# Odd-layer values in six chunks of 512 weight columns instead of eight of 384

## The chip, the cores and the metric

The kernel runs on one core of one Trainium2 chip. The metric is the device time of one execution in microseconds (us), the median of three timed runs. The engines are named as in the profile: PE is TensorE's matmuls, PEld its weight loads, DVE is VectorE, ACT ScalarE, POOL GpSimd, SP the engine that issues nearly all DMAs.

## The reference

A two-layer encoder trunk on 256 tokens of width 1024, float32. The even layer has neighbourhood and latent attention, the odd layer a mixture of dilated windows; each is followed by a squared-ReLU MLP. Cut to the odd layer, which is the one that changes:

```python
def odd_mixer(xn, w_in, w_o, cos_f, sin_f):
    b, s, _ = xn.shape
    hcat = (xn @ w_in).reshape(b, s, DIL_GROUPS, 3, DIL_HEADS, HEAD_DIM)
    q = apply_rope(hcat[:, :, :, 0], cos_f, sin_f)
    k = apply_rope(hcat[:, :, :, 1], cos_f, sin_f)
    v = hcat[:, :, :, 2]
    return dilated_attention(q, k, v) @ w_o
```

`DIL_GROUPS` is 3 (window patterns), `DIL_HEADS` 16 heads of 64. For each head, `dilated_attention` takes a softmax in each of the three groups over the keys of that group's window and combines the three by their softmax denominators, which is the same as one softmax over all three groups' scores side by side.

## The kernel before

**Products in two parts.** A float32 weight comes by DMA into a tile `raw` (`load_weight`, L138). ScalarE rounds it into `whi` (L176) and VectorE writes the rest `raw - whi` into `wlo` (L177), in four pieces per weight. Activations are held as such pairs too. A product is then three matmuls, high times high, high times low, low times high (`mm3`, L179 to L182), or two, where high and low of the activation lie side by side as 512 columns (`mm2`, L184 to L187: one of 512 columns and one of 256). The weights of the whole trunk stand in one list, `specs`; `weight()` (L167) hands out the next one, loads four ahead and splits two ahead. There are four `raw` buffers and three pairs `whi`/`wlo`.

**The odd layer** (`odd`, L782) works in eight units of two heads. For each unit u:

- `qk_steps` (L823): three weights of 1 MB, b = 0, 1, 2: queries and keys of group 0; then queries of groups 1 and 2; then their keys. Each b has four steps (f, half) of four `mm2` pairs; a bank `acc` of the accumulation memory holds the result of one f, 128 weight columns, and `joined` (L191: a copy on ScalarE, an add on VectorE, L193 and L194) takes it out. Behind the fourth step stands `rope`: four small DMAs on SP swap the halves, and VectorE multiplies and adds (L847 to L853). The results are the tiles `q0` (group 0), `q12` and `k12`.
- `value_steps` (L798): two weights of 768 KB. Per block of 128 tokens 24 matmuls of 384 columns (8 parts of the depth, three matmuls each) sum up in one bank; `out` (L813) takes the 384 columns out, scaled: 128 by VectorE into `v0`, twice 128 by ScalarE into `v12`.
- `attention` (L863): `scores` puts the group 0 scores (`two_heads`, L201, with `q0`) and those of groups 1 and 2 (L878, with `q12` and `k12`) into four banks `w`, then, for each of four pairs (i, j) of token block and head, reduces and subtracts on VectorE (L886), takes exponentials and scales on ScalarE (L890, L892). `turn` (L895) transposes the probabilities `pp` on TensorE (L899, three matmuls) and copies them out as `pts` (L901, on ScalarE or VectorE).
- `mix` (L906): the transposed probabilities times `v0` and `v12` (L914, L919), into one bank `acc`, split into `oa` or `ob` for the output product.

The loop over u from 2 to 7 (L936) weaves the product steps of unit u with the attention of unit u - 1, into which the mix of unit u - 2 is put behind the scores: twelve steps of queries and keys, then four of values, and beside them scores, two empty steps, and the four turns with an empty step behind each. `weave` (L203) spreads the second list over the first in proportion to their lengths. "Unit u's loop" is below what the weave of unit u's products holds, with the attention of unit u - 1. Unit 0 has no attention beside it; in unit 1's loop the attention of unit 0 starts three steps late; the attention of unit 7 stands beside the output product (L943), which opens four banks `acc` at once.

**What sets the order.** The code lists the steps, but a scheduler lays down each engine's queue when the program is built: it keeps the order of the code where an instruction is ready by its own estimate, and puts later ones ahead of one that it takes to be late. Each engine then runs its queue in that order, waiting on counts of the other engines. There are four banks `acc` and four banks `w`; a new tile takes a bank whose last reader is through.

Of the kernel before, what the change touches and what calls it, by code (L numbers as in the profile page):

```python
# [39 lines left out]
WPARTS = 4  # L40
NORM_PRIO = 300


@with_exitstack
def trunk(ctx, tc, a, out):
# [82 lines left out]
    for u in range(8):  # L128
        ov = [(a["w_ov"][u, j], 4 * 384) for j in range(2)]
        oqk = [(a["w_oqk"][u, j], WCH) for j in range(3)]  # L130
        specs.extend(oqk + ov if u else ov + oqk)
# [47 lines left out]
    def mm3(o, sh, sl, mh, ml, first, last):  # L179
        nc.tensor.matmul(o, sh, mh, start=first, stop=False)  # L180
        nc.tensor.matmul(o, sh, ml, start=False, stop=False)  # L181
        nc.tensor.matmul(o, sl, mh, start=False, stop=last)  # L182
# [29 lines left out]
    def tok(t):  # L212
        return slice(t * P, (t + 1) * P)
# [568 lines left out]
    def odd(op, xT, s):  # L782
# [8 lines left out]
        def unit_tiles(u):  # L791
            d = {}
            for n, shape, dt in (("q0", [P, 2, 2, T], F32R), ("q12", [P, 2, T], F32), ("k12", [P, 2, T], F32),
                                 ("v0", [P, NT, P], F32), ("v12", [P, 4, P], F32)):
                d[n] = op.tile(shape, dt, tag=n, name=n, bufs=2)
            return d

        def value_steps(d):  # L798

            wt, acc = [], {}  # L800

            def gemm(i, half):
                if len(wt) <= half:
                    wt.append(weight())
                if half == 0:
                    acc[i] = bank("acc")
                pq = acc[i]
                wh, wl = wt[half]
                for k in range(4):
                    ws = slice(k * 384, k * 384 + 384)  # L810
                    kk = 4 * half + k
                    mm3(pq[:, 0:384], xh[:, kk, tok(i)], xl[:, kk, tok(i)], wh[:, ws], wl[:, ws], kk == 0, kk == KT - 1)
            def out(i):  # L813
                pq, ri = acc[i], column(r[0], i)
                nc.vector.tensor_scalar(d["v0"][:, i, :], pq[:, 0:P], ri, None, ALU.mult)
                for c in range(2):
                    rows = slice(64 * c, 64 * c + 64)
                    nc.scalar.activation(d["v12"][0:64, 2 * i + c, :], pq[rows, P:2 * P], AF.Copy, scale=ri[rows])
                    nc.scalar.activation(d["v12"][64:P, 2 * i + c, :], pq[rows, 2 * P:3 * P], AF.Copy, scale=ri[rows])

            return [lambda i=i, h=h: gemm(i, h) for i in range(NT) for h in range(2)], [lambda i=i: out(i) for i in range(NT)]
# [34 lines left out]

        def all_values(d):
            g, o = value_steps(d)
            return [g[0], lambda: run_all([g[1], o[0]]), g[2], lambda: run_all([g[3], o[1]])]

# [44 lines left out]

        def mix(u, d, out_tag):  # L906
            pvo = bank(out_tag)
            for i in range(NT):
                pts = [turned.pop((u, i, j)) for j in range(2)]
                at = i * P  # L910
                for kk in range(NT):
                    for j in range(2):
                        cs = slice(64 * j, 64 * j + 64)
                        nc.tensor.matmul(pvo[cs, tok(i)], d["v0"][:, kk, cs], pts[j][:, kk, :], start=kk == 0, stop=False)  # L914
                for c in range(2):
                    qs = slice(64 * c, 64 * c + 64)
                    for j in range(2):
                        cs = slice(64 * j, 64 * j + 64)
                        nc.tensor.matmul(pvo[cs, at + 64 * c:at + 64 * c + 64], d["v12"][:, 2 * i + c, cs], pts[j][:, 2, qs],  # L919
                                         start=False, stop=c == 1)  # L920
            split(*halves(mixed[u // 4][:, u % 4]), pvo[:, 0:T])

        d, nd = unit_tiles(0), unit_tiles(1)
        v0, v_out = value_steps(d)
        run_all(v0)
        r = [rstd(s)]
# [7 lines left out]
        run_all(first[2:])  # L934
        weave(qk_steps(nd) + all_values(nd), attention(0, d, lambda: None, 3), 3)
        for u in range(2, 8):  # L936
            pd, d, nd = d, nd, unit_tiles(u)
            side = attention(u - 1, d, lambda: mix(u - 2, pd, "acc"))

            weave(qk_steps(nd) + all_values(nd), side + [lambda: mix(6, d, "acc")] if u == 7 else side)  # L940
        accs, wo = open_accs(), {}
        side = attention(7, nd, lambda: None) + [lambda: mix(7, nd, "w")]
        weave([f for k in range(6) for f in out_steps(accs, mixed, wo, k)], side)  # L943
# [54 lines left out]
def _layout(i):  # L998
# [56 lines left out]
```

## Time and profile before

| what | value |
|---|---|
| median of three runs | 745.56 us (745.47 to 745.57) |
| profiled execution | 745.33 us, its span 743.5 us |
| granted TensorE clock, mean | 0.998 |
| odd layer's units 2 to 6 | from 350.5 to 499.5 us of the span, 29.8 us each |
| loads of value weights | 16 of 768 KB, 4.7 us each to landing |
| loads of query and key weights | 24 of 1 MB, 5.1 us each to landing |

A row of groups reads: line, engine, operation, written tile, read tiles, shape, count; then busy time, mean of one in ns, and idle time ahead of it with what ended it. A row of the timeline reads: start and length in us, engine, line, operation, tiles, shape, count, and in brackets the engine's idle time just before and what ended it. A row of the windows reads: the stretch, its length, then busy time of PE, PEld, DVE, ACT and POOL with their counts, granted clock, share of the DMA engines, GB/s. Matmul records overlap, since the next one starts before the last has drained.

### The profile page before, as it was taken

Reading aid. Unit: us, or ns where it says so; the run is one execution under the profiler, and the core shown is the slowest. Engines: PE = TensorE matmul, PEld = TensorE weight load, DVE = VectorE, ACT = ScalarE, POOL = GpSimd, SP = SyncE. Lnnn points to the kernel's source line nnn. Section 1 sums busy time; section 2 is a strip of 40 time slices with the busy share of each in tenths; the row PEclk is TensorE's granted clock in tenths of the full one; section 3 lists DMA queues with packets and bytes.
Section 4 is the critical chain, followed back from the end, with each engine's and each line's share of the span. In section 5 each row is a group of like instructions: output and inputs, shape, how many; then the busy total and the mean of one; then the engine's idle time right before and its main releaser. Section 6 shows DMA issues by size and latency. Waiting matters only on the chain.

```text
span 743.5 us, 12706 instructions
## 1 busy us (share of the span) xinstructions
PE 735.2 (99%) x4764; PEld 644.6 (87%) x4764; DVE 550.1 (74%) x1248; ACT 463.4 (62%) x1038; POOL 6.1 (1%) x16
## 2 busy tenths in 40 slices
PE   8999999999999999999999999999999999999996
PEld 6898998888888888989899899898998888888885
DVE  6699849666666666998888988888869665665664
ACT  6679977454454556758676766867667554554541
POOL 0100000000000000000000000000000000000000
PEclk9999999999999999999999999999999999999999
DMA  8866334554464554575655455456653655555401
GB/s 283 340 210 223 114 114 160 183 224 173 171 222 174 174 191 149 189 242 171 199 207 183 164 194 196 165 177 225 216 199 121 218 171 201 176 191 192 178 26 56
DMA packets 28108, 136.88 MB, mean 184 GB/s; under 512 B 4496, under 2 KB 7056, under 8 KB 14992
## 3 DMA queue, kind: packets, MB, share of 16 engines
q1 hardware_dynamic: 27760, 135.81, 53.0%
q8 instruction: 37, 0.61, 0.3%
q10 hardware_dynamic: 288, 0.28, 0.1%
q14 instruction: 23, 0.19, 0.1%
HBM read 127.68 MB, written 1.05 MB: 173 GB/s over the span
## 4 chain that ended last, share of the span: by engine, by line
PE 95%; DMA 1%; issue 1%; DVE 0%; SPq 0%; ACT 0%; POOLq 0%; POOL 0%; DVEq 0%
PE w L186 16%; PE acc L180 14%; PE acc L181 14%; PE acc L182 14%; PE acc L186 12%; PE w L187 8%; PE acc L187 6%; PE w L201 1%; PE w L899 1%; PE w L714 1%; PE acc L914 1%; DMA raw<-in_w_v 1%; PE w L729 1%; PE w L878 1%; DMA raw<-in_w_c 1%
## 5 line engine op out<-in xcount | busy, mean ns | idle before, releaser
L177 DVE TENSOR_TENSOR wlo<-raw,whi 128x512 fp32r<-128x512 f32 (+3 forms) x488 | 304.1, 663 | 75.6 <-ACT whi L176 74.0
L176 ACT CAST whi<-raw 128x512 fp32r<-128x512 f32 (+3 forms) x488 | 264.2, 602 | 81.1 <-issue 70.3
L186 PE MATMUL w<-xT,whi 128*128 128x512 f32 x512 | 179.3, 394 | 0.0
L186 PE MATMUL acc<-xT,whi 128*128 128x512 f32 x384 | 137.3, 401 | 0.0
L187 PE MATMUL w<-xT,wlo 128*128 128x256 f32 x512 | 132.8, 280 | 0.0
L186 PEld LDWEIGHTS w<-xT,whi 128*128 128x128 f32 x512 | 93.6, 187 | 18.3
L187 PEld LDWEIGHTS w<-xT,wlo 128*128 128x128 f32 x512 | 96.1, 188 | 5.5
L187 PE MATMUL acc<-xT,wlo 128*128 128x256 f32 x384 | 99.8, 280 | 0.0
L180 PE MATMUL acc<-whi,h 128*128 128x512 f32 x250 | 98.4, 393 | 0.0
L181 PE MATMUL acc<-wlo,h 128*128 128x512 f32 x250 | 97.8, 391 | 0.0
L182 PE MATMUL acc<-whi,h 128*128 128x512 f32 x250 | 97.4, 390 | 0.0
L186 PEld LDWEIGHTS acc<-xT,whi 128*128 128x128 f32 x384 | 70.0, 188 | 12.7
L193 ACT COPY up<-w 128x256 f32<-128x256 f32 x64 | 23.9, 374 | 88.4 <-PE w L186 88.4
L187 PEld LDWEIGHTS acc<-xT,wlo 128*128 128x128 f32 x384 | 72.2, 188 | 3.7
L194 DVE TENSOR_TENSOR up<-up,w 128x256 f32<-128x256 f32 x64 | 26.8, 419 | 63.0 <-ACT up L193 62.2
L180 PE MATMUL acc<-whi,xT 128*128 128x384 f32 (+2 forms) x160 | 56.5, 353 | 0.6 <-ACT whi L176 0.6
L181 PE MATMUL acc<-wlo,xT 128*128 128x384 f32 (+2 forms) x160 | 56.0, 350 | 0.3 <-DVE wlo L177 0.3
L182 PEld LDWEIGHTS acc<-whi,h 128*128 128x128 f32 x250 | 46.9, 188 | 10.2
L181 PEld LDWEIGHTS acc<-wlo,h 128*128 128x128 f32 x250 | 47.0, 188 | 9.8
L182 PE MATMUL acc<-whi,xT 128*128 128x384 f32 (+2 forms) x160 | 55.4, 346 | 0.0
L180 PEld LDWEIGHTS acc<-whi,h 128*128 128x128 f32 x250 | 46.9, 188 | 9.1
L181 PEld LDWEIGHTS acc<-wlo,xT 128*128 128x128 f32 x160 | 30.2, 189 | 3.1 <-DVE wlo L177 2.1
(195 smaller groups left out, 1043.6 us busy)
## 6 DMA issues: line engine op xcount, KB each, us to landing
raw<-in_w SPq DMA_DIRECT2D x64, 1024.0 KB, 4.8
raw<-in_w_oqk SPq DMA_DIRECT2D x24, 1024.0 KB, 5.1
raw<-in_w_ov SPq DMA_DIRECT2D x16, 768.0 KB, 4.7
sw<-qk SPq DMA_DIRECT2D x96, 64.0 KB, 3.2
raw<-in_w_qk SPq DMA_DIRECT2D x4, 1024.0 KB, 11.0
raw<-in_w_oe SPq DMA_DIRECT2D x4, 1024.0 KB, 5.7
raw<-in_w_oo SPq DMA_DIRECT2D x4, 1024.0 KB, 5.5
bias<-in_rpb SPq DMA_DIRECT2D x8, 256.0 KB, 4.2
```

The source lines that it names most:

```text
L176: a = nc.scalar.copy(hi, src).ins
L177: return a, (eng or nc.vector).tensor_tensor(lo, src, hi.bitcast(F32), op=ALU.subtract).ins
L180: nc.tensor.matmul(o, sh, mh, start=first, stop=False)
L181: nc.tensor.matmul(o, sh, ml, start=False, stop=False)
L182: nc.tensor.matmul(o, sl, mh, start=False, stop=last)
L186: both = lambda: nc.tensor.matmul(o, sh, m.rearrange("p v n -> p (v n)"), start=first, stop=last)
L187: low = lambda: nc.tensor.matmul(o[:, 0:T], sl, m[:, 0, :], start=False, stop=False)
L193: nc.scalar.copy(dst, o[:, T:2 * T])
L194: nc.vector.tensor_tensor(dst, dst, o[:, 0:T], op=ALU.add)
L201: nc.tensor.matmul(o[j], qk[pb, 0, a, ts], qk[pb, 1, b, :], start=n == 0, stop=n == 2)
L714: nc.tensor.transpose(pt[:, b * P:(b + 1) * P], pp[:, b // 2, (b % 2) * P:(b % 2 + 1) * P], ident)
L729: nc.tensor.matmul(pvo[64 * j:64 * j + 64, tok(t)], v[:, kk, h * 64:(h + 1) * 64], pts[:, 2 * j + kk, :], start=kk == 0, stop=kk == NT - 1)
```

## The change

The value weights of all eight units, 3072 columns, are laid side by side: unit 0's three groups, unit 1's, and so on, 24 blocks of 128. They are cut into six chunks of 512 columns (four blocks). A chunk is two weights of 1 MB, and its product per token block is 24 matmuls of 512 columns in one bank. Chunk c holds blocks 4c to 4c + 3, and so parts of two units. The table `OV_CHUNKS` says which loop makes which chunk: units 0, 1, 2, 4, 5, 6 make one each, units 3 and 7 none. The tiles `v0` and `v12` therefore no longer belong to a unit's set: `unit_values` opens them when a chunk first writes to a unit, from a ring of four instead of two, and `mix` takes them out.

```diff
+OV_CHUNKS = ((0,), (1,), (2,), (), (3,), (4,), (5,), ())
...
-        ov = [(a["w_ov"][u, j], 4 * 384) for j in range(2)]
+        ov = [(a["w_ov"][c, j], WCH) for c in OV_CHUNKS[u] for j in range(2)]
...
-            for n, shape, dt in (("q0", [P, 2, 2, T], F32R), ("q12", [P, 2, T], F32), ("k12", [P, 2, T], F32),
-                                 ("v0", [P, NT, P], F32), ("v12", [P, 4, P], F32)):
+            for n, shape, dt in (("q0", [P, 2, 2, T], F32R), ("q12", [P, 2, T], F32), ("k12", [P, 2, T], F32)):
...
-        def value_steps(d):
+        values = {}
+
+        def unit_values(u):
+            if u not in values:
+                values[u] = [op.tile(shape, F32, tag=n, name=n, bufs=4) for n, shape in (("v0", [P, NT, P]), ("v12", [P, 4, P]))]
+            return values[u]
+
+        def value_steps(chunk):
...
-                    ws = slice(k * 384, k * 384 + 384)
+                    ws = slice(k * 512, k * 512 + 512)
                     kk = 4 * half + k
-                    mm3(pq[:, 0:384], xh[:, kk, tok(i)], xl[:, kk, tok(i)], wh[:, ws], wl[:, ws], kk == 0, kk == KT - 1)
+                    mm3(pq, xh[:, kk, tok(i)], xl[:, kk, tok(i)], wh[:, ws], wl[:, ws], kk == 0, kk == KT - 1)
...
-                nc.vector.tensor_scalar(d["v0"][:, i, :], pq[:, 0:P], ri, None, ALU.mult)
-                for c in range(2):
-                    rows = slice(64 * c, 64 * c + 64)
-                    nc.scalar.activation(d["v12"][0:64, 2 * i + c, :], pq[rows, P:2 * P], AF.Copy, scale=ri[rows])
-                    nc.scalar.activation(d["v12"][64:P, 2 * i + c, :], pq[rows, 2 * P:3 * P], AF.Copy, scale=ri[rows])
+                for n in range(4):
+                    u, g = divmod(4 * chunk + n, 3)
+                    (v0, v12), cs = unit_values(u), slice(n * P, n * P + P)
+                    if g == 0:
+                        nc.vector.tensor_scalar(v0[:, i, :], pq[:, cs], ri, None, ALU.mult)
+                    else:
+                        for c in range(2):
+                            rows = slice(64 * c, 64 * c + 64)
+                            nc.scalar.activation(v12[64 * g - 64:64 * g, 2 * i + c, :], pq[rows, cs], AF.Copy, scale=ri[rows])
...
-        def all_values(d):
-            g, o = value_steps(d)
-            return [g[0], lambda: run_all([g[1], o[0]]), g[2], lambda: run_all([g[3], o[1]])]
+        def all_values(u):
+            steps = []
+            for c in OV_CHUNKS[u]:
+                g, o = value_steps(c)
+                steps += [g[0], lambda g=g, o=o: run_all([g[1], o[0]]), g[2], lambda g=g, o=o: run_all([g[3], o[1]])]
+            return steps
...
-        def mix(u, d, out_tag):
-            pvo = bank(out_tag)
+        def mix(u, out_tag):
+            pvo, (v0, v12) = bank(out_tag), values.pop(u)
...
-            weave(qk_steps(nd) + all_values(nd), side + [lambda: mix(6, d, "acc")] if u == 7 else side)
+            weave(qk_steps(nd) + all_values(u), side + [lambda: mix(6, "acc")] if u == 7 else side)
...
-    d["w_ov"] = f(wo[:, :, 2].reshape(2, 4, P, 3, 8, P).transpose(4, 0, 2, 1, 3, 5).reshape(8, 2, P, 4 * 384))
+    ov = wo[:, :, 2].reshape(D, 3, 8, P).transpose(0, 2, 1, 3)
+    d["w_ov"] = f(ov.reshape(2, 4, P, 6, 512).transpose(3, 0, 2, 1, 4).reshape(6, 2, P, WCH))
```

The new file's lines stand one lower up to the value steps (L176 becomes L177) and 14 lower in the attention (L878 becomes L892, L899 becomes L913). The change moves instructions at places that its diff does not name. The first is unit 4's loop on TensorE, with the attention of unit 3. Before, `w_4654` and `w_4655` are score banks, `acc_4686` is the mix of unit 2, the banks `acc_4645` to `acc_4893` are unit 4's queries and keys, `w_4811` and the other L899 are the four turns:

```order
L201 MATMUL w_4654<-q0_4237 128x256
...
L878 MATMUL w_4654<-k12_4239,q12_4238 64x64
...
L914 MATMUL acc_4686<-pts_4425,v0_3850 64x128
...
L186 MATMUL acc_4759<-xT_3053,whi_4564 128x512
...
L186 MATMUL acc_4802<-xT_3053,whi_4634 128x512
...
L899 MATMUL w_4811<-ident_87,pp_4706 128x128 x3
...
L899 MATMUL w_4855<-ident_87,pp_4717 128x128 x3
L186 MATMUL acc_4874<-xT_3053,whi_4791 128x512
...
L899 MATMUL w_4902<-ident_87,pp_4728 128x128 x3
...
L899 MATMUL w_4981<-ident_87,pp_4739 128x128 x3
```

The same place now; `w_4578` is a score bank, `acc_4610` the mix, `acc_4569` (whose first half stands ahead of the scores), `acc_4683`, `acc_4726`, `acc_4751` and `acc_4798` are unit 4's queries and keys in their order:

```order
L202 MATMUL w_4578<-q0_4249 128x256
...
L928 MATMUL acc_4610<-pts_4413,v0_3812 64x128
...
L187 MATMUL acc_4683<-xT_3053,whi_4489 128x512
...
L187 MATMUL acc_4726<-xT_3053,whi_4558 128x512
...
L892 MATMUL w_4578<-k12_4251,q12_4250 64x64
...
L187 MATMUL acc_4751<-xT_3053,whi_4558 128x512
...
L913 MATMUL w_4735<-ident_87,pp_4630 128x128 x3
L188 MATMUL acc_4751<-xT_3053,wlo_4559 128x256 x2
L187 MATMUL acc_4751<-xT_3053,whi_4558 128x512
L913 MATMUL w_4779<-ident_87,pp_4641 128x128 x3
L913 MATMUL w_4826<-ident_87,pp_4652 128x128 x3
L187 MATMUL acc_4798<-xT_3053,whi_4715 128x512
```

The scores of groups 1 and 2 stood directly behind those of group 0; now the mix, the rest of `acc_4569`, `acc_4683` and half of `acc_4726` stand between them. Between those scores and the first turn stood the mix and 32 product matmuls, now 21 product matmuls; between the turns stood 24, 24 and 32, now 3 and none, and the fourth comes behind the first value block. The product into `acc_4798` waits for a count of VectorE that is reached with the add that reads `acc_4569`. That add (L195) stands on VectorE in this place, with what is ahead of it; `pts_4783` and `pts_4830` are the copies of the second and third turn, `wlo_4854` is the low part of a value weight, `drz_4655` and `drz_4666` belong to the third and fourth softmax:

```order
L905 RECIPROCAL drz_4655<-dz_4654 128x1
L915 COPY pts_4783<-w_4779 128x384
L900 ISA sn_4662,dmn_4664<-w_4581,mask_3183,dmn_4664 128x64
L900 ISA dmn_4664 128x1
L178 TENSOR_TENSOR wlo_4854<-raw_4713,whi_4853 128x512
L915 COPY pts_4830<-w_4826 128x384
L178 TENSOR_TENSOR wlo_4854<-raw_4713,whi_4853 128x512
L905 RECIPROCAL drz_4666<-dz_4665 128x1
L195 TENSOR_TENSOR qk_4568<-qk_4568,acc_4569 128x256
```

Before, the same stretch of VectorE had no copy of a second and third turn in it; the add is the last row:

```order
L891 RECIPROCAL drz_4731<-dz_4730 128x1
L886 ISA sn_4738,dmn_4740<-w_4657,mask_3183,dmn_4740 128x64
L886 ISA dmn_4740 128x1
L177 TENSOR_TENSOR wlo_4864<-raw_4632,whi_4863 128x384
L891 RECIPROCAL drz_4742<-dz_4741 128x1
L901 COPY pts_4815<-w_4811 128x384
L194 TENSOR_TENSOR qk_4644<-qk_4644,acc_4645 128x256
```

The add of the first bank now stands behind the copy of the third turn, which itself needs the third softmax. The other place is VectorE in unit 1's loop, ahead of the first scores of groups 1 and 2; `qk_3493` (now `qk_3495`) is unit 0's last join, `k12_3191` its rotated keys. Before:

```order
L194 TENSOR_TENSOR qk_3493<-qk_3493,acc_3513 128x256
L848 TENSOR_TENSOR sw_3472<-sw_3472,sinT_3182 128x512
L177 TENSOR_TENSOR wlo_3688<-raw_3481,whi_3687 128x384
L853 TENSOR_TENSOR k12_3191<-r1_3473,sw_3472 128x512
L847 TENSOR_TENSOR r1_3533<-qk_3493,cosT_3181 128x512
```

And now:

```order
L195 TENSOR_TENSOR qk_3495<-qk_3495,acc_3515 128x256
L178 TENSOR_TENSOR wlo_3690<-raw_3483,whi_3689 128x512
L859 TENSOR_TENSOR sw_3474<-sw_3474,sinT_3182 128x512
L178 TENSOR_TENSOR wlo_3690<-raw_3483,whi_3689 128x512
L864 TENSOR_TENSOR k12_3191<-r1_3475,sw_3474 128x512
```

A split piece of 384 columns between the join and the keys has become two of 512. On TensorE the scores that read these keys stand five product matmuls later than before (12 of `acc_3634` ahead of them instead of 7 of `acc_3632`), and 20 products instead of 25 lead from them to the first turn. Beside the output product, the scores of unit 7's groups 1 and 2 stand 46 product matmuls behind those of group 0 instead of directly behind them, and the turns have 31, 10, 10 and 20 matmuls ahead of them instead of 36, 24, 24 and 24.

More of the change, by code (lines that the diff above doesn't have):

```diff
@@ L913, in mix @@
                         cs = slice(64 * j, 64 * j + 64)
-                        nc.tensor.matmul(pvo[cs, tok(i)], d["v0"][:, kk, cs], pts[j][:, kk, :], start=kk == 0, stop=False)
+                        nc.tensor.matmul(pvo[cs, tok(i)], v0[:, kk, cs], pts[j][:, kk, :], start=kk == 0, stop=False)
                 for c in range(2):
@@ L918, in mix @@
                         cs = slice(64 * j, 64 * j + 64)
-                        nc.tensor.matmul(pvo[cs, at + 64 * c:at + 64 * c + 64], d["v12"][:, 2 * i + c, cs], pts[j][:, 2, qs],
+                        nc.tensor.matmul(pvo[cs, at + 64 * c:at + 64 * c + 64], v12[:, 2 * i + c, cs], pts[j][:, 2, qs],
                                          start=False, stop=c == 1)
@@ L923, in odd @@
         d, nd = unit_tiles(0), unit_tiles(1)
-        v0, v_out = value_steps(d)
-        run_all(v0)
+        products, v_out = value_steps(0)
+        run_all(products)
         r = [rstd(s)]
@@ L934, in odd @@
         run_all(first[2:])
-        weave(qk_steps(nd) + all_values(nd), attention(0, d, lambda: None, 3), 3)
+        weave(qk_steps(nd) + all_values(1), attention(0, d, lambda: None, 3), 3)
         for u in range(2, 8):
-            pd, d, nd = d, nd, unit_tiles(u)
-            side = attention(u - 1, d, lambda: mix(u - 2, pd, "acc"))
-            weave(qk_steps(nd) + all_values(nd), side + [lambda: mix(6, d, "acc")] if u == 7 else side)
+            d, nd = nd, unit_tiles(u)
+            side = attention(u - 1, d, lambda: mix(u - 2, "acc"))
+            weave(qk_steps(nd) + all_values(u), side + [lambda: mix(6, "acc")] if u == 7 else side)
         accs, wo = open_accs(), {}
-        side = attention(7, nd, lambda: None) + [lambda: mix(7, nd, "w")]
+        side = attention(7, nd, lambda: None) + [lambda: mix(7, "w")]
         weave([f for k in range(6) for f in out_steps(accs, mixed, wo, k)], side)
```

## The prediction

> **What bounds the kernel now.** I read the page first, then the windows of the odd layer, then the timeline of single engines inside one unit. Busy time, clock and the chain that ended last stand in these rows of the page:
>
> ```profile
> PE 735.2 (99%) x4764; PEld 644.6 (87%) x4764; DVE 550.1 (74%) x1248; ACT 463.4 (62%) x1038; POOL 6.1 (1%) x16
> PEclk9999999999999999999999999999999999999999
> PE 95%; DMA 1%; issue 1%; DVE 0%; SPq 0%; ACT 0%; POOLq 0%; POOL 0%; DVEq 0%
> ```
>
> TensorE is the bound from end to end: it carries 95% of the chain. The windows over units 2 and 3 of the odd layer say the same of the stage that is changed:
>
> ```profile
> 350.50:380.30 29.80, 29.80 (x233) 27.08 (x232) 24.85 (x71) 20.98 (x51) 0.00 (x0) 1.00 0.57 186
> 380.30:410.10 29.80, 29.80 (x233) 27.09 (x232) 25.23 (x71) 21.22 (x51) 0.00 (x0) 1.00 0.57 186
> ```
>
> In 29.8 us TensorE has no gap, VectorE is busy 25 us, ScalarE 21 us, DMA 57%. So only two things can move the time: how long TensorE's own instructions take, and whether TensorE comes to wait. What VectorE, ScalarE and the DMAs gain or lose counts only as a wait of TensorE.
>
> **The change part by part.**
>
> **A, the products.** 384 matmuls of 384 columns become 288 of 512: the same 147,456 columns in 96 instructions fewer. Their recorded time is no price:
>
> ```profile
> L180 PE MATMUL acc<-whi,xT 128*128 128x384 f32 x128 | 44.0, 343 | 0.0
> 370.30 0.34 PE L180 MATMUL acc<-whi,xT 128*128 128x384 f32 x1
> 374.36 0.34 PE L182 MATMUL acc<-whi,xT 128*128 128x384 f32 x1
> 375.21 0.34 PE L182 MATMUL acc<-whi,xT 128*128 128x384 f32 x1
> 378.85 0.34 PE L182 MATMUL acc<-whi,xT 128*128 128x384 f32 x1
> L180 PE MATMUL acc<-whi,h 128*128 128x512 f32 x250 | 98.4, 393 | 0.0
> 20.40 0.39 PE L181 MATMUL acc<-wlo,xT 128*128 128x512 f32 x1
> 28.36 0.39 PE L182 MATMUL acc<-whi,xT 128*128 128x512 f32 x1
> 722.20 0.40 PE L180 MATMUL acc<-whi,h 128*128 128x512 f32 x1
> 726.06 0.39 PE L182 MATMUL acc<-whi,h 128*128 128x512 f32 x1
> ```
>
> A record lasts 343 ns, but they overlap: what counts is the distance of starts. From 370.30 to 374.36 are 23 steps, 0.1765 us each (a first token's block straight behind the query and key products); from 375.21 to 378.85 are 21 steps, 0.1733 us each (a block behind transposes). Five blocks of 24 are of the first sort (units 2 to 6), eleven of the second: 5 x 24 x 0.1765 + 11 x 24 x 0.1733 = 21.2 + 45.8 = 67.0 us. For 512 columns there are two prices. The even layer's value product, with the same operands, takes (28.36 - 20.40) / 34 = 0.2341 us; the MLP's down product takes (726.06 - 722.20) / 17 = 0.2271 us. 288 of them are 67.4 or 65.4 us, so A is +0.4 or -1.6 us. The first is nearest in its operands, the second is by far the longer run (250 on each of its three lines); I take the middle, **-0.6 us**.
>
> [...]
>
> **Other engines.** The splits of these weights go from 64 pieces of 384 to 48 of 512 on both engines, with as many columns; the copies out stay 16 on VectorE and 64 on ScalarE. TensorE hides both as long as no product waits for them. The loads keep their bytes (16 x 768 KB, now 12 x 1 MB). The ring of four costs no wait: unit 4's values, the first that reuse a buffer, are written two units after the mix that read unit 0's.
>
> **B, unit 4's loop.** Unit 3 now ends with its key product, and the scheduler answers: in unit 4's loop the score matmuls of groups 1 and 2 (L878 before, L892 now) stand behind the mix and 32 more products, and three of the four turns follow with three products between them. How long the softmax takes between them I read in unit 2's loop, before the change (TensorE, then ScalarE, then VectorE):
>
> ```profile
> 351.64 0.69 PE L878 MATMUL w<-k,q 64*64 64x64 f32 x32
> 352.27 0.66 PE L914 MATMUL acc<-pts,v 128*64 128x128 f32 x8
> 359.49 0.49 PE L899 MATMUL w<-ident,pp 128*128 128x128 f32 x3
> 359.73 0.48 PE L186 MATMUL acc<-xT,whi 128*128 128x512 f32 x1
> 379.03 0.40 PE L186 MATMUL acc<-xT,whi 128*128 128x512 f32 x1
> 379.27 0.28 PE L187 MATMUL acc<-xT,wlo 128*128 128x256 f32 x1
> 380.08 0.39 PE L186 MATMUL acc<-xT,whi 128*128 128x512 f32 x1
> ...
> 356.16 0.62 ACT L892 ACTIVATE pp<-pp,drz 128x384 f32<-128x384 f32 x1 [0.23 <-DVE drz L891]
> 357.62 0.62 ACT L892 ACTIVATE pp<-pp,drz 128x384 f32<-128x384 f32 x1 [0.23 <-DVE drz L891]
> 359.14 0.61 ACT L892 ACTIVATE pp<-pp,drz 128x384 f32<-128x384 f32 x1
> 360.77 0.62 ACT L892 ACTIVATE pp<-pp,drz 128x384 f32<-128x384 f32 x1
> ...
> 353.14 0.41 DVE L886 CUSTOM_DVE_ANT_0 sn<-w,mask 128x256 f32<-128x256 f32 x1
> 353.49 0.68 DVE L177 TENSOR_TENSOR wlo<-raw,whi 128x512 fp32r<-128x512 f32 x1
> 354.09 0.28 DVE L886 CUSTOM_DVE_ANT_0 sn<-w,mask,dmn 128x64 f32<-128x64 f32 x1
> 360.39 0.16 DVE L891 RECIPROCAL drz<-dz 128x1 f32<-128x1 f32 x1 [0.56 <-ACT pp L890]
> 360.47 0.54 DVE L901 COPY pts<-w 128x384 f32<-128x384 f32 x1
> 360.92 0.74 DVE L194 TENSOR_TENSOR qk<-qk,acc 128x256 f32<-128x256 f32 x2
> ```
>
> The scores end at 352.27. The first reduction starts at 353.14, behind three split pieces, and 3.64 us later, at 356.78, the first probabilities are there; the next follow 1.46, 1.51 and 1.64 us apart. The first transpose stood at 359.49, 2.7 us after its operand: it did not wait. A pair of products (512 and 256 columns) takes (380.08 - 379.03) / 3 = 0.35 us, its wide part 0.24, its narrow part 0.11; a group of three transposes costs 0.33 us (0.24 to the next start, and that one is some 0.09 late). Now, from the end of the scores:
>
> 1. 8 + 13 products stand before the first turn: 4 pairs, then 7 wide and 6 narrow, 1.40 + 2.34 = 3.75 us. Its operand comes 3.64 us after the first reduction, which starts 0.1 (VectorE free) to 0.87 us (as before) after the scores: 3.75 to 4.5. Wait 0 to 0.75, I take 0.4.
> 2. Two narrow products and one wide stand before the second: 0.33 + 0.47 = 0.8 us, against 1.46 to 1.64: wait 0.65 to 0.85, I take 0.75.
> 3. Nothing stands before the third: 0.33 us against the same: wait 1.15 to 1.3, I take 1.25.
> 4. The next product, into acc_4798, waits for VectorE to have read acc_4569. On VectorE stand, behind the third transpose (0.49 us to its end): its copy out (0.45, the distance of starts from 360.47 to 360.92), a split piece (0.60, from 353.49 to 354.09), a reciprocal (0.1) and the add (0.41, half of 0.74 and its latency); with 0.1 for handing over 2.15 us, against 0.33. Wait 1.5 (the piece done before) to 2.0, I take 1.8.
>
> Behind each wait stand all later matmuls, so the whole wait reaches the end. B is **+4.2 us** (3.3 to 4.9).
>
> **C, unit 1's loop.** Here the scores already waited for the rotated key:
>
> ```profile
> 328.16 0.69 DVE L853 TENSOR_TENSOR k<-r,sw 128x512 f32<-128x512 f32 x1
> 328.90 0.69 PE L878 MATMUL w<-k,q 64*64 64x64 f32 x32 [0.19 <-DVE k L853]
> ```
>
> On VectorE two split pieces of 512 (0.60 each) now stand between the last join and the key where one of 384 stood, some 0.75 us more; on TensorE the scores stand five products, 0.9 us, later: about even, a wait up to 0.4 us. Then 20 products, 3.5 us, instead of 25 lead to the first transpose, against 3.64 us and more. I take **+0.6 us** (0 to 1.1).
>
> **D, unit 7 and the output product.** Here too the scores moved back, but more work is left between the transposes:
>
> ```profile
> 532.68 0.38 PE L180 MATMUL acc<-oa,whi 128*128 128x256 f32 x1
> 537.12 0.55 PE L899 MATMUL w<-ident,pp 128*128 128x128 f32 x3
> ```
>
> 36 products took 4.44 us; now 31 stand there, 3.8 us, against 3.75 to 4.5. The next turns have 10, 10 and 20 products of 0.12 us between them, 1.2 us and more with 0.33 for the transposes, against 1.46 to 1.64: hardly a wait. I take **+0.2 us** (0 to 0.7).
>
> **Sum.** -0.6 + 4.2 + 0.6 + 0.2 = +4.4 us. The profiled execution took 745.33 us (its span of 743.5 and 1.8 around it), 0.23 us under the median of 745.56; the sum gives 749.73 us on that execution and 749.96 on the median, and I say **749.8 us**.
>
> **The rivals.**
>
> *Faster or no change: the softmax keeps up.* If in unit 4's loop the first probabilities come within 3.75 us of the scores and the next at 0.8 us or less, B, C and D vanish, and A alone is left: 743.9 to 746.0 us. For it: the mix no longer falls between these reductions. Against it: the spacing is that of ScalarE, two passes of 0.6 us for each, which the change leaves as they are. It decides from a spacing of 0.8 us, about half of what the rows show. 8%, half of it under 745.56 by over 0.2%.
>
> *More waits.* Unit 7's end goes like unit 3's, with a wait at each of the four turns and at the first output banks: up to 3 us over D, 752.4 to 753 us. For it: the same cause. Against it: the 10 products between the turns. 9%.
>
> *The clock falls.* In unit 4's loop TensorE would work only some 1.5 of 5.7 us (4.2 us of waits, and 0.33 + 0.8 + 0.33 of work between them). If the granted clock fell to half for 4 us there, the products in them would take about 2 us more: some 752 us. Against it: it stood at 1.00 in 9 to 16 us too, where the start waits for weights:
>
> ```profile
> 9.00:16.00 7.00, 7.00 (x36) 6.22 (x35) 6.96 (x15) 5.96 (x14) 0.00 (x0) 1.00 0.88 314
> ```
>
> 4%. [...]
>
> **How the numbers follow.** The forecast case (waits at units 4 and 1, 746.9 to 752.4 us) has 79%. Of its ends the low one is A at -1.6, B at 3.3, nothing else: 747.3; the high one all upper ends, 752.7. The range 747.2 to 752.4 leaves out the first rival and part of the others, some 18%. What a measurement of this kernel can tell from no change is about 0.2%, 1.5 us. Faster by more than that: 4%; within it: 8%; slower: 88%.
>
> **What would show it.** In the changed profile the four waits must stand on L913 and the following L187 in one stretch of some 5 us in unit 4's loop, released by ScalarE (pp) and VectorE (qk), 0.4, 0.75, 1.25 and 1.8 us. The starts of the 512-column products lie 0.227 to 0.234 us apart. A loop with values lasts 29.8 + 48 x (0.2306 - 0.1749) = 32.5 us, those of units 3 and 7 some 21.4 without their waits. I am wrong if L913 shows no wait in unit 4, or if the time went into the value products themselves.

## The result and the profile after

The changed kernel took **754.66 us** (median of 4 runs, 753.43 to 755.96) against 745.52 us (4 runs, 745.47 to 745.57): a ratio of 1.0124, 95% interval 1.0112 to 1.0135. The forecast was 749.8 us, the range ended at 752.4. The runs of the kernel before differ by 0.1 us, those of the changed kernel by 2.5; that has to be explained too. All times here and below are of runs in the fast state; one slow run of e5, 1029.67 us at a mean clock of 0.655, is left out.

The profiled execution took 753.43 us, 8.1 us more than the profiled one of before (745.33). These are the rows of its page that answer to those shown of before (busy time, clock, chain):

```profile
PE 739.8 (98%) x4668; PEld 634.3 (84%) x4668; DVE 552.6 (74%) x1235; ACT 459.4 (61%) x1019; POOL 5.7 (1%) x16
PEclk9999999999999999999999999999999999999999
PE 86%; DVE 4%; DMA 3%; ACT 3%; issue 2%; SPq 1%; POOLq 0%; POOL 0%; DVEq 0%; ACTq 0%
```

The chain, 95% TensorE before, is now 86% TensorE, with VectorE, DMA and ScalarE in it: TensorE waits for them somewhere. The clock row, in 40 slices, shows nothing; it is too coarse. The windows over whole loops of the odd layer (from one unit's first score matmul to the next) find the place. First the kernel before, units 1, 2 and 4 and the stretch from unit 7's scores to the next norm; then the changed kernel, units 1 to 5 and the last stretch. The columns are length, then busy time of PE, PEld, DVE, ACT and POOL, granted clock, DMA share, GB/s.

```profile
326.24:350.74 24.50, 24.31 (x179) 21.86 (x178) 21.59 (x64) 17.86 (x43) 0.00 (x0) 1.00 0.64 221
350.74:380.53 29.79, 29.79 (x234) 27.08 (x233) 24.84 (x70) 20.96 (x50) 0.00 (x0) 1.00 0.57 186
410.32:440.12 29.80, 29.80 (x235) 27.09 (x234) 25.14 (x70) 21.30 (x51) 0.00 (x0) 1.00 0.56 186
531.14:574.32 43.18, 43.18 (x365) 40.56 (x365) 35.50 (x86) 28.61 (x63) 0.00 (x0) 1.00 0.51 182
```

```profile
329.16:357.21 28.05, 27.60 (x177) 22.54 (x176) 24.02 (x65) 19.20 (x46) 0.00 (x0) 1.00 0.62 211
357.21:389.83 32.62, 32.62 (x234) 27.71 (x234) 27.66 (x72) 22.92 (x54) 0.00 (x0) 1.00 0.56 186
389.83:411.21 21.38, 21.38 (x185) 18.61 (x184) 17.59 (x53) 16.50 (x40) 0.00 (x0) 1.00 0.53 173
411.21:449.92 38.71, 35.22 (x233) 28.79 (x233) 29.75 (x77) 20.68 (x48) 0.00 (x0) 0.96 0.50 164
449.92:482.53 32.61, 32.61 (x233) 27.71 (x232) 27.47 (x71) 22.41 (x53) 0.00 (x0) 1.00 0.57 186
538.25:582.36 44.11, 43.95 (x366) 40.65 (x366) 37.03 (x89) 26.64 (x58) 0.00 (x0) 1.00 0.53 184
```

- Products: a loop with a wide chunk is 32.62 - 29.79 = 2.83 us longer, one without is 29.79 - 21.38 = 8.41 us shorter. Six and two of them: 6 x 2.83 - 2 x 8.41 = **+0.2 us**.
- Unit 4's loop: 38.71 - 32.62 = **+6.1 us** over a loop with the same work. By the profile TensorE is idle for 38.71 - 35.22 = 3.5 us of it, and the mean clock is 0.96.
- Unit 1's loop: 28.05 - 24.50 - 2.83 = **+0.7 us**.
- The last stretch: 44.11 - 43.18 = **+0.9 us**.

Together 7.9 of the 8.1 us; 0.2 us are there before the loops. Inside unit 4's loop the timeline of TensorE shows the four waits, and something else behind them:

```profile
423.80 0.39 PE L187 MATMUL acc<-xT,whi 128*128 128x512 f32 x1
424.30 0.55 PE L913 MATMUL w<-ident,pp 128*128 128x128 f32 x3
424.61 0.48 PE L188 MATMUL acc<-xT,wlo 128*128 128x256 f32 x2
424.92 0.40 PE L187 MATMUL acc<-xT,whi 128*128 128x512 f32 x1
425.93 0.55 PE L913 MATMUL w<-ident,pp 128*128 128x128 f32 x3 [0.61 <-ACT pp L906]
427.56 0.55 PE L913 MATMUL w<-ident,pp 128*128 128x128 f32 x3 [1.07 <-ACT pp L906]
429.74 0.79 PE L187 MATMUL acc<-xT,whi 128*128 128x512 f32 x1 [1.64 <-DVE qk L195]
430.33 0.41 PE L188 MATMUL acc<-xT,wlo 128*128 128x256 f32 x1
430.55 0.63 PE L187 MATMUL acc<-xT,whi 128*128 128x512 f32 x1
430.97 0.41 PE L188 MATMUL acc<-xT,wlo 128*128 128x256 f32 x1
```

By starts, less 0.24 us for a product of 512 columns and 0.33 for three transposes, the waits are 424.30 - 423.80 - 0.24 = 0.26, 0.77, 427.56 - 425.93 - 0.33 = 1.30 and 1.85 us, 4.2 us together. A fifth, small one stands ahead of the scores of groups 1 and 2, which need unit 3's rotated keys: they start at 419.55 us, 0.33 behind a product of 256 columns that takes 0.12, so 0.2 us. Behind the fourth wait a pair of products takes 430.97 - 430.33 = 0.64 us, where it takes 0.35 elsewhere. Narrow windows around this place show why:

```profile
426.02:429.43 3.41, 1.01 (x6) 0.53 (x6) 2.71 (x9) 3.41 (x10) 0.00 (x0) 1.00 0.18 72
429.43:432.84 3.41, 3.10 (x9) 2.67 (x10) 3.41 (x8) 1.80 (x5) 0.00 (x0) 0.50 0.23 58
432.84:436.25 3.41, 3.41 (x21) 2.96 (x20) 1.80 (x4) 0.37 (x1) 0.00 (x0) 1.00 0.39 96
```

For 3.41 us the granted clock is one half: 9 matmuls where the next 3.41 us hold 21. In the 3.41 us ahead of that TensorE was busy for 1.01 us only.

### The profile page after: what moved, and what is told of

Its sections match the earlier page's. It is cut to its first block, busy times and chain, and to the rows that moved or that the text cites. A ratio compares the mean times of both kernels' runs of the same rounds, so it can differ in the third digit from the quotient of the medians.

```text
span 751.7 us, 12461 instructions
## 1 busy us (share of the span) xinstructions
PE 739.8 (98%) x4668; PEld 634.3 (84%) x4668; DVE 552.6 (74%) x1235; ACT 459.4 (61%) x1019; POOL 5.7 (1%) x16
## 4 chain that ended last, share of the span: by engine, by line
PE 86%; DVE 4%; DMA 3%; ACT 3%; issue 2%; SPq 1%; POOLq 0%; POOL 0%; DVEq 0%; ACTq 0%
PE w L187 16%; PE acc L181 14%; PE acc L182 14%; PE acc L183 14%; PE w L188 8%; PE acc L187 8%; PE acc L188 4%; DMA raw<-in_w_c 1%; DVE wlo L178 1%; DMA sw<-qk 1%; PE w L202 1%; ACT pp L904 1%; PE w L715 1%; PE w L913 1%; PE w L730 1%
## 5 line engine op out<-in xcount | busy, mean ns | idle before, releaser
L178 DVE TENSOR_TENSOR wlo<-raw,whi 128x512 fp32r<-128x512 f32 (+2 forms) x472 | 302.6, 680 | 68.7 <-ACT whi L177 67.5
L177 ACT CAST whi<-raw 128x512 fp32r<-128x512 f32 (+2 forms) x472 | 263.3, 617 | 92.9 <-issue 78.0
L187 PE MATMUL acc<-xT,whi 128*128 128x512 f32 x384 | 139.5, 404 | 1.6 <-DVE qk L195 1.6
L195 DVE TENSOR_TENSOR up<-up,w 128x256 f32<-128x256 f32 x64 | 26.8, 419 | 63.0 <-ACT up L194 62.3
L181 PE MATMUL acc<-whi,xT 128*128 128x512 f32 (+1 forms) x128 | 51.5, 402 | 0.4 <-ACT whi L177 0.2
L182 PE MATMUL acc<-wlo,xT 128*128 128x512 f32 (+1 forms) x128 | 51.1, 399 | 0.3 <-DVE wlo L178 0.3
L183 PE MATMUL acc<-whi,xT 128*128 128x512 f32 (+1 forms) x128 | 50.8, 397 | 0.0
L830 ACT ACTIVATE v<-acc,rstd 64x128 f32<-64x128 f32 x64 | 23.2, 363 | 17.5 <-PE acc L183 15.0
```

Source lines behind the costliest of these rows:

```text
L177: a = nc.scalar.copy(hi, src).ins
L178: return a, (eng or nc.vector).tensor_tensor(lo, src, hi.bitcast(F32), op=ALU.subtract).ins
L187: both = lambda: nc.tensor.matmul(o, sh, m.rearrange("p v n -> p (v n)"), start=first, stop=last)
L195: nc.vector.tensor_tensor(dst, dst, o[:, 0:T], op=ALU.add)
L830: nc.scalar.activation(v12[64 * g - 64:64 * g, 2 * i + c, :], pq[rows, cs], AF.Copy, scale=ri[rows])
```

## The experiments

The theory after the result: the softmax waits are as forecast; what was missed is mostly the half clock that follows from TensorE's idleness, and which some runs get for longer than others. The rivals: the wide products draw the clock down or are slow themselves; or the loss is elsewhere. The kernel before ran beside every kernel, on the same chip.

| run | us, median (lowest to highest) | ratio to before (95%) |
|---|---|---|
| e6, the changed kernel again | 755.42 (754.31 to 756.10) | 1.0134 (1.0120 to 1.0148) |
| e1, unit 4's attention later | 748.40 (747.25 to 748.77) | 1.0039 (1.0026 to 1.0051) |
| e2, waits filled | 751.49 (751.29 to 751.76) | 1.0083 (1.0069 to 1.0097) |
| e7, two waits filled | 751.32 (750.98 to 752.78) | 1.0084 (1.0070 to 1.0098) |
| e8, last wait filled | 751.86 (751.35 to 752.88) | 1.0092 (1.0077 to 1.0108) |
| e3, 384 columns, unit 3 empty | 750.93 (749.79 to 751.58) | 1.0072 (1.0059 to 1.0086) |
| e5, 384 columns, unit 7 empty | 745.58 (745.25 to 746.07) | 1.0004 (0.9995 to 1.0013) |
| e4, e1 with banks alternating | 747.53 (747.51 to 748.44) | 1.0032 (1.0020 to 1.0045) |
| e9, e1 with xT 160 bytes on | 746.41 (745.60 to 747.26) | 1.0016 (1.0007 to 1.0025) |
| e10, before, xT 160 bytes on | 743.72 (743.09 to 744.42) | 0.9979 (0.9970 to 0.9988) |
| e11, before, xT 96 bytes on | 743.35 (743.17 to 744.26) | 0.9977 (0.9968 to 0.9986) |
| e12, before, xT 192 bytes on | 742.04 (741.62 to 742.60) | 0.9957 (0.9944 to 0.9969) |

### The waits taken away (e1)

```diff
-            weave(qk_steps(nd) + all_values(u), side + [lambda: mix(6, "acc")] if u == 7 else side)
+            weave(qk_steps(nd) + all_values(u), side + [lambda: mix(6, "acc")] if u == 7 else side, 2 if u == 4 else 0)
```

> The changed kernel; in unit 4's loop alone the attention steps are dealt out over the products with a lead of two steps, so that scores and turns come later. Nothing else moves. Theory (the loss is the idle time of TensorE in unit 4's loop and the half clock that follows it): the waits of L913 and L187 there go (at most 0.5 us is left of 4.3), the clock stays at 1.00 in that loop, the runs lie within 0.5 us of each other, and the time is 745.5 + 0.2 (products) + 0.7 (unit 1) + 0.9 (output) + 0.3 = 747.6 us (746.8 to 748.5). Rival 1 (the wide products themselves or their load pull the clock down): the waits go but the clock still falls somewhere in units 4 to 6, the runs still differ by 2 us, 748.5 to 751 us. Rival 2 (the loss is elsewhere): over 751 us.

Measured: 748.40 us. The windows over the loops of units 3 and 4 (here the border between them lies 2.8 us later in the work):

```profile
389.77:413.97 24.20, 24.20 (x202) 21.07 (x202) 20.76 (x59) 18.03 (x43) 0.00 (x0) 1.00 0.53 173
413.97:444.23 30.26, 30.26 (x218) 25.23 (x218) 26.01 (x71) 18.77 (x43) 0.00 (x0) 1.00 0.55 180
```

TensorE is busy throughout at a clock of 1.00, and the two loops take 54.46 us, against 21.38 + 38.71 = 60.09 in the changed kernel; 21.38 + 32.62 = 54.00 would be no loss at all. So 5.6 of the 6.1 us of unit 4's loop hang on its waits, and the wide products alone do not bring the clock down. What is left over the kernel before, 2 us in the profiled execution (747.25) and 3.1 in the medians, fits the other three terms in the first; the runs of e1 and of the kernel before on this chip each spread by over 1 us, so the rest isn't assigned.

### The waits kept, the idleness taken away (e2, e7, e8)

```diff
+        def fill(o, n):
+            for _ in range(n):
+                nc.tensor.transpose(o[:, 0:P], ident, ident)
...
                 pt = bank("w")
+                fill(pt, {(0, 1): 6, (1, 0): 11}.get((i, j), 0) if u == 3 else 0)
...
+                if (u, i, j) == (3, 1, 0):
+                    fill(bank("w"), 16)
```

Only the added lines are shown. e2 is this; e7 has the first `fill` alone, e8 the second alone.

> The changed kernel with 33 idle transposes of the identity put into three of the waits of unit 4's loop: 6 ahead of the second turn of unit 3's attention, 11 ahead of the third, 16 behind it. They take 0.11 us each and compute nothing that is used. Theory (idle time of TensorE brings the clock down): the time lost to the softmax stays, but TensorE is busy in it, so the clock stays at 1.00 and the 1.4 us and more that the half clock cost go: 751.5 to 752.8 us, and the runs lie within 0.5 us of each other. Rival (the clock falls for another cause, such as the wide products or the DMAs): 753.4 to 756 us, runs 2 us apart, and a stretch at half clock in the profile. Rival 2 (the slow products after 429.7 us are not the clock): as the rival, with the clock at 1.00.

> As e2 with the 6 and 11 idle transposes ahead of the second and third turn alone; the wait of 1.9 us behind the third turn stays idle. Theory (the clock falls when a whole stretch of some 3.4 us was mostly idle; a single wait of 1.9 us leaves over 40% of it busy): clock 1.00, 751.3 to 752.3 us as e2. Rival (one long wait is enough): a half-clock stretch behind that wait, 753 us and more.

> As e2 with the 16 idle transposes behind the third turn alone; the waits of 0.3, 0.8 and 1.3 us ahead of the turns stay idle, 2.4 us in a stretch of 3.6 us. Theory (mostly idle stretch): this lies at the edge, so some runs fall and some don't: runs 1 to 2 us apart between 751.3 and 754 us. Rival (only the last, longest wait brings the clock down): 751.3 to 752.3 us, runs within 0.5 us. Rival 2 (any idle time does): all runs over 752.5 us.

> The changed kernel unaltered, on the same chip as the runs beside it. Theory: 754 to 756 us, the runs 1 to 3 us apart, with one to three stretches of 3.41 us at half clock in unit 4's loop (in the first profile one, 429.43 to 432.84 us). Rival (its first runs were a chance of that chip): below 752.5 us or runs within 0.5 us.

In e2 TensorE's timeline has the idle transposes (L879) where the waits were; the turns (L918) and the next product start about as far apart as in the changed kernel, 426.02 - 424.39 = 1.63, 1.62 and 2.10 us (there 1.63, 1.63 and 2.18):

```profile
424.39 0.55 PE L918 MATMUL w<-ident,pp 128*128 128x128 f32 x3
424.69 0.48 PE L188 MATMUL acc<-xT,wlo 128*128 128x256 f32 x2
425.01 0.40 PE L187 MATMUL acc<-xT,whi 128*128 128x512 f32 x1
425.25 0.82 PE L879 MATMUL w<-ident 128*128 128x128 f32 x6
426.02 0.55 PE L918 MATMUL w<-ident,pp 128*128 128x128 f32 x3
426.41 1.36 PE L879 MATMUL w<-ident 128*128 128x128 f32 x11
427.64 0.55 PE L918 MATMUL w<-ident,pp 128*128 128x128 f32 x3
428.03 1.80 PE L879 MATMUL w<-ident 128*128 128x128 f32 x15
429.74 0.50 PE L187 MATMUL acc<-xT,whi 128*128 128x512 f32 x1
```

The windows view over unit 4's loop, in e2:

```profile
410.73:448.63 37.90, 37.17 (x267) 31.24 (x266) 30.39 (x77) 20.59 (x48) 0.00 (x0) 1.00 0.50 167
```

in e7:

```profile
410.91:448.50 37.59, 35.51 (x252) 29.52 (x251) 29.90 (x77) 20.69 (x48) 0.00 (x0) 1.00 0.51 169
```

in e8:

```profile
410.91:448.42 37.51, 35.55 (x249) 29.37 (x249) 29.92 (x76) 20.58 (x48) 0.00 (x0) 1.00 0.51 169
```

and in e6, the unaltered kernel:

```profile
412.14:452.40 40.26, 36.44 (x233) 29.80 (x232) 29.62 (x76) 20.67 (x48) 0.00 (x0) 0.92 0.48 158
```

Useless work in the waits makes the kernel faster: e2 takes 751.49 us and its runs lie within 0.5 us, where the unaltered kernel took 754.66 and, in e6, 755.42. The clock is 1.00 in the three filled ones. Filling a part of the waits is enough: with 17 transposes (e7) or 16 (e8) the loop is no longer than in e2, and three of four runs stay below 752.2 us. One run of each, 752.78 and 752.88 us, is slower; whether the clock fell in it no profile shows (its mean of 0.996 is the lowest of its kernel, but runs of the kernel before have that too). So neither one long wait (the last, left idle in e7) nor the others without it (e8) brought the clock down in the profiled executions. For e6 the narrow windows around the waits, as for the first profile:

```profile
426.61:430.03 3.42, 1.09 (x6) 0.62 (x6) 2.64 (x11) 3.42 (x10) 0.00 (x0) 1.00 0.31 127
430.03:433.44 3.41, 2.45 (x7) 2.13 (x8) 3.41 (x9) 2.44 (x7) 0.00 (x0) 0.50 0.15 38
433.44:436.85 3.41, 3.41 (x12) 2.86 (x11) 0.89 (x2) 0.34 (x1) 0.00 (x0) 0.50 0.39 97
436.85:440.26 3.41, 3.41 (x20) 2.94 (x19) 2.02 (x4) 0.74 (x3) 0.00 (x0) 1.00 0.85 288
```

There are two stretches of 3.41 us at half clock, not one. The first of them still holds 0.96 us of the last wait (it began at 430.03, with the wait still on); in the first profile the stretch began later in that wait, held 0.31 us of it, and full clock followed. For e7 and then e8, one window of the same length over the waits:

```profile
425.91:429.32 3.41, 2.27 (x19) 1.82 (x17) 2.76 (x11) 3.41 (x11) 0.00 (x0) 1.00 0.21 84
425.31:428.72 3.41, 1.92 (x16) 1.69 (x17) 2.63 (x11) 3.41 (x10) 0.00 (x0) 1.00 0.28 115
```

TensorE was busy for 67% and 56% of them, and the clock stayed at 1.00; behind 30% (first profile) and 32% (e6) it fell to 0.50. A window begun elsewhere holds another share. Over what stretch TensorE's work sets the clock, and below what share it falls, no run shows, nor why one run of e8 was slower.

The loops also differ in the wait for the rotated keys, in e6 420.80 - 420.15 - 0.12 = 0.53 us:

```profile
420.15 0.28 PE L188 MATMUL acc<-xT,wlo 128*128 128x256 f32 x1
420.80 0.70 PE L892 MATMUL w<-k,q 64*64 64x64 f32 x32 [0.37 <-DVE k L864]
```

By starts it is 0.2 us in the first profile, 0.6 in e7 and 0.3 in e8. Less this wait, unit 4's loop takes 38.5 us with one stretch at half clock, 39.7 with two, and 37.1 (the mean of e7 and e8) with none: one stretch costs **1.4 us**, two cost **2.6 us**. The pace says the same: pairs of 0.64 instead of 0.35 us lose 45% of the time worked at half clock, which is 1.4 us of 3.10 and 2.6 us of 2.45 + 3.41.

The two profiled executions of the changed kernel (753.43 and 755.87 us) lie 2.4 us apart: 1.5 in this loop, 1.2 of it by the clock, and 0.9 ahead of it, where it begins at 411.21 and at 412.14 us. The mean clock of the other runs points the same way: 0.997 in the fastest of the first four, 0.992 and 0.993 in the other three. Of the 3.9 us between the medians of e6 and e2 this loop holds 2.4 in the profiled executions (40.26 - 37.90); 1.4 lie ahead of it (it begins at 410.73 us in e2) and were not followed up.

### The width and the empty units apart (e3, e5)

Both go back to eight chunks of 384 columns and empty one unit each; the rest is as in the changed kernel. The first added table is e3's, the second e5's; the lines that set the width back to 384 in the product and the weights are not shown.

```diff
-OV_CHUNKS = ((0,), (1,), (2,), (), (3,), (4,), (5,), ())
+OV_CHUNKS = ((0,), (1,), (2, 3), (), (4,), (5,), (6,), (7,))
...
+OV_CHUNKS = ((0,), (1,), (2,), (3,), (4,), (5,), (6, 7), ())
...
-                for n in range(4):
-                    u, g = divmod(4 * chunk + n, 3)
+                for n in range(3):
+                    u, g = chunk, n
```

> Eight chunks of 384 columns as in the kernel before, one for each unit, but the chunk of unit 3 is made in unit 2's loop behind that of unit 2 (value tiles in a ring of four), so unit 3 makes none. Theory (the empty unit is the cause, not the width): three waits and a stretch at half clock in unit 4's loop as in the changed kernel, none elsewhere: 745.5 + 3.4 to 4.5 of waits + 1.4 to 3.9 of clock = 750.3 to 754 us. Rival (the wide products are the cause): within 0.5 us of the kernel before, clock 1.00.

> Eight chunks of 384 columns, one for each unit, but unit 7's is made in unit 6's loop behind that of unit 6, so unit 7 alone makes none. Theory (the +0.9 us between unit 7 and the output is the price of an empty unit 7, as the first output products and the scores of the last unit come closer together): 0.6 to 1.2 us slower than before, 746.0 to 746.6 us, no wait over 0.4 us. Rival (that stretch is slower because of the wide products or the half clock ahead of it): within 0.3 us of before.

e3 took 750.93 us: the loss of unit 4's loop comes with 384 columns as well. Its windows, the whole loop and the two stretches around the fall of the clock:

```profile
410.59:445.73 35.14, 32.35 (x234) 28.19 (x234) 25.41 (x70) 18.37 (x45) 0.00 (x0) 0.95 0.51 164
424.70:428.12 3.42, 1.10 (x7) 0.62 (x6) 2.84 (x11) 3.42 (x11) 0.00 (x0) 1.00 0.15 62
428.12:431.53 3.41, 3.20 (x10) 2.71 (x11) 3.30 (x8) 1.71 (x5) 0.00 (x0) 0.50 0.26 61
```

35.14 - 29.80 = 5.3 us over the kernel before, so the empty unit 3 is the cause, not the width. e5 is within 0.1% of before: an empty unit 7 costs some 0.3 us, which the interval doesn't tell from nothing, and less than the 0.6 to 1.2 expected. Its last stretch took 43.48 us, 0.3 more than before's 43.18; the changed kernel's 44.11 holds 0.6 more that e5 doesn't have. The view of waits gives 0.2 us of it to VectorE (`ob`, L178); whether the wide chunks set that wasn't tried.

### The pace of the wide products (e4, e9)

```diff
-                    mm3(pq, xh[:, kk, tok(i)], xl[:, kk, tok(i)], wh[:, ws], wl[:, ws], kk == 0, kk == KT - 1)
+                    for i in range(NT):
+                        mm3(acc[i], xh[:, kk, tok(i)], xl[:, kk, tok(i)], wh[:, ws], wl[:, ws], kk == 0, kk == KT - 1)
```

Only the product is shown; the order of the steps changes with it, and both blocks are taken out behind the last step.

> As e1, and in the odd layer's value products the two token blocks alternate inside the loop over k, three products into one bank and then three into the other, as in the MLP's down product, where before all 24 products of a token block ran into one bank. Theory (the pace of 0.227 us in the down product comes from its changing banks): starts 0.227 apart instead of 0.234, 288 x 0.007 = 2.0 us faster than e1, some 745.5 us. Rival (the pace hangs on the stationary operand or on something else that the two products differ in): 0.234 as before, within 0.5 us of e1.

The pace stayed at 0.234 us with two banks, so the banks are not it (the time, 747.53 us, is 0.1% under e1's, within the intervals). The next difference between the two products is where the stationary operand lies in SBUF, the memory of the tiles. In the program these tiles take whole multiples of 2 KB of a partition each, and bytes are counted here and in the expectations as the remainder of the address by that size: the MLP's `h` begins at byte 1504, as the weights do, and `xT` at 1344. It is a way to tell the addresses apart; whether the pace goes by this remainder is the question. e9 moves `x` and `xT` by 160 bytes and changes no instruction. It also moves, by 160 or 96 bytes, all that lies between `x` and the two small tiles: the attention outputs `oa`, `ob` and `c` and nearly all working tiles (`pp`, `up`, `hsq`, most `qk`). The weights, `h` and the odd layer's `q0`, `q12`, `k12`, `v0`, `v12` stay:

```diff
-        ms = work.tile([P, NT], F32, tag="ms", name="ms")
+        ms = const.tile([P, NT], F32, tag="ms", name="ms", bufs=2)
...
-            mn, z, rz = (work.tile([P, 2], F32, tag=v, name=v, bufs=3) for v in ("mn", "z", "rz"))
+            mn, z, rz = ((const if v == "z" else work).tile([P, 2], F32, tag=v, name=v, bufs=3) for v in ("mn", "z", "rz"))
```

> As e1, with every instruction the same on every engine; two small tiles (ms and z, 160 bytes of a partition in all) are taken from the first pool instead of a later one, so that x and xT begin 160 bytes further on and all later tiles stay where they were. Before, xT begins at byte 1344 of a 2 KB line, the weight pieces whi and wlo and the MLP's h at byte 1504; now all at 1504. Theory (the value products' 0.234 us comes from where xT lies against the weights): their starts come 0.227 apart, 288 x 0.007 = 2.0 us faster than e1, ratio to before about 1.001 instead of 1.004, and the pairs of query and key products may become faster too. Rival (the place in SBUF is nothing to the pace): 0.234 as before, the time of e1 within 0.7 us.

First and last of 23 value products of a token block behind transposes, the changed kernel and then e9:

```profile
475.66 0.40 PE L182 MATMUL acc<-wlo,xT 128*128 128x512 f32 x1
480.80 0.40 PE L183 MATMUL acc<-whi,xT 128*128 128x512 f32 x1
```

```profile
468.92 0.39 PE L182 MATMUL acc<-wlo,xT 128*128 128x512 f32 x1
473.93 0.39 PE L183 MATMUL acc<-whi,xT 128*128 128x512 f32 x1
```

(480.80 - 475.66) / 22 = 0.2336 us, and (473.93 - 468.92) / 22 = 0.2277. The theory holds for these products: the same instructions, the MLP's pace, and a ratio to before of 1.0016 instead of 1.0039; of what they read, only `xT` moved. Even so the wide chunks stay 0.16% slower than the kernel before, and 2.7 us slower than e10 below, which has the same move (746.41 against 743.72 us).

### The same move on the kernel before (e10, e11, e12)

The edits are e9's (e10), `z` alone (e11), and `mn` and `z` (e12), with all instructions as in the kernel before.

> The kernel before with the same move of x and xT by 160 bytes, all instructions unchanged. Theory (place of xT): the five blocks of 24 products of 384 columns that ran at 0.1765 us run at 0.1733, and the even layer's value product at 0.227 instead of 0.234: 0.4 + 48 x 0.007 = 0.7 us faster, up to 3 us if the pairs of 512 and 256 columns are faster too. Rival: within 0.4 us of before.

> As e10, the kernel before with x and xT moved, but by 96 bytes only: xT begins at byte 1440 of a 2 KB line, the weights at 1504. All instructions unchanged. Theory (the pace needs xT at the same place of a line as the weights): products of the even layer's value product at 0.234 us and the five blocks behind the pairs at 0.1765 as before, the time of before within 0.4 us. Rival (only some places, that of before among them, are slow): 0.227 and 0.1735, some 1.5 us faster, as e10.

> As e10, moved by 192 bytes: xT begins at byte 1536, 32 bytes behind the place of the weights. Theory (same place needed): as before, within 0.4 us. Rival (any place from 1504 on, or most places, do): 0.227 and 0.1735, some 1.5 us faster.

All three are faster than both kernels, e12 the most: 742.04 us, 0.43% under before. The value products behind the pairs, 0.1765 us before, took 0.1736 in e10 and e11 and 0.1741 in e12. But the theory that `xT` must lie at the weights' place falls: 96 and 192 bytes do it too. Nor is there one order of good and bad places: the even layer's value product, 0.2341 us before, took 0.2276, 0.2294 and 0.2330 us in e10, e11 and e12, so e12 is slowest there of the three and fastest in all. The value products hold only a part of the gain (e10: 120 x 0.0029 + 48 x 0.0065 = 0.7 of 1.4 us). The traces say more when the distances from each product's start to the next start are added up by what it reads:

| products that read | before, us | e10 | e11 | e12 |
|---|---|---|---|---|
| `xT` | 434.29 | 433.97 | 433.77 | 431.64 |
| `oa` or `ob` | 47.78 | 47.72 | 46.20 | 46.96 |
| `h` | 176.17 | 175.48 | 175.75 | 176.11 |
| first to last start | 736.09 | 735.02 | 733.97 | 732.87 |

In e11 1.6 of 2.1 us lie in the output products, whose `oa` and `ob` moved too: in the odd layer they start 0.120 us apart before (541.31 to 543.47 us, 18 steps) and 0.114 in e11 (539.41 to 541.69 us, 20 steps). In e12 2.7 of 3.2 us lie in the products of `xT`. In e10 0.7 of 1.1 us lie in those of `h`, which did not move, nor did their weights. So the place of a product's own operands cannot be all of it; what other engines read and write beside it moved as well, and no run takes the two apart. By what rule the place sets the pace stays open.

## Why the prediction was wrong

- **What bounds it:** right. Every loss is TensorE's own pace or its waits.
- **A, the products:** forecast -0.6 us, measured +0.2, inside the bounds of -1.6 to +0.4. The choice that failed is the middle between two prices: the one with the same operands (0.2341 us) was right to within 0.3%, and e9 shows that a price from another tile need not carry over even with equal shapes. That more products ran at the other price was no reason to lean to it.
- **B, unit 4's loop:** the waits were right, each of them: 0.4, 0.75, 1.25, 1.8 us forecast, 0.26, 0.77, 1.30, 1.85 measured. The loop lost 6.1 us all the same: 4.2 in these, 1.4 to the clock (one stretch), 0.2 in the wait for the rotated keys (0.5 in e6), which the forecast put at nothing, and 0.3 that isn't split further.
- **The rival "the clock falls":** this is the step that failed: the sum had no term for the clock. The rival was given 4% and is what happened in both profiled executions of the changed kernel; in the six other runs the mean clock, 0.992 or 0.993, points the same way. It was priced at about 2 us, which was good, and cost 1.4 (one stretch) to 2.6 (two). The half that the price took is what the trace of before shows too, but only behind its last matmul: 0.50 from 742 us on. The reason against it was bad: the row of 9 to 16 us was quoted as a place with waits at a clock of 1.00, but it shows TensorE busy in 7.00 of 7.00 us, so it says nothing of idleness. And the forecast's own numbers had TensorE at work in 1.5 of 5.7 us. What stands ahead of the fall is not one long wait but several: 2.40 of 3.41 us idle in the first profile. In e7 the longest wait was left idle and in e8 the others; the windows shown were idle for 33 and 44%, and the clock stayed at 1.00.
- **C, unit 1's loop:** +0.6 forecast, +0.7 measured, but half of that by luck. By starts the scores wait 0.1 us longer than before and the first turn 0.14, as the forecast had in mind. The other 0.4 us stand ahead of the first value product (343.45 to 344.09 us, before 340.24 to 340.48), where it had nothing; what this one waits for the view of waits doesn't show.
- **D, unit 7 and output:** +0.2 forecast, +0.9 measured, over the upper bound of 0.7. The empty unit makes 0.3 of it (e5); the rest is not assigned.
- **Sum:** for the profiled execution 0.8 (A) + 1.4 (clock) + 0.5 (keys and rest of B) + 0.1 (C) + 0.7 (D) + 0.2 (ahead of the loops) = 3.7 us over 749.73, that is 753.43. Without the clock it would have been 752.0, inside the range. The median is 1.2 us higher; three of the four runs have the lower mean clock, as in e6, where a second stretch cost that much. (All upper ends of the forecast's own terms came to 752.7, above the 752.4 that it gave as the end of the range.)

## What to carry to other kernels

When a change makes TensorE wait several times within a few microseconds, add the waits up; don't look at the longest alone. Here the clock fell to 0.50 behind 3.41 us that were 30 to 32% busy (first profile, e6, e3), and stayed at 1.00 behind 3.41 us that were 56 and 67% busy (e8, e7); where TensorE comes as low as the first, price a half clock behind it, here 1.4 us for one stretch and 2.6 for two, and expect runs to scatter, here by 2.5 us. Before a unit of work is emptied, look at what its products cover in the next unit, and move the waiting steps back with it (e1: one number, some 6 us). A price for a matmul is taken from the same operands first; an equal shape from another tile differed by 3% here (0.2341 and 0.2271 us).

## What was not expected of the hardware

- Moving `x`, `xT`, the attention outputs and the working tiles by 96 to 192 bytes in SBUF, with all instructions, the weights and `h` where they were, made the kernel before 0.21 to 0.43% faster; a move by 160 bytes brought the starts of the wide products from 0.2336 to 0.2277 us apart.
- Transposes that compute nothing (33, 3.6 us) kept the clock up and made the changed kernel 3.2 us (first runs) to 3.9 us (e6) faster, 2.4 of it in unit 4's loop.
- After one stretch of 3.41 us at half clock that TensorE worked 3.10 us of, full clock came back; after one that it worked 2.45 us of, a second stretch at half clock followed.
